# Filler matrix products around the first modulation rows of a one-core transformer step

## The chip, the cores and the metric

The kernel runs on one NeuronCore of one Trainium2 chip. A core has a tensor engine for matrix products (PE; its weight loads are listed apart as PEld), a vector engine (DVE), a scalar engine (ACT), a general engine (GpSimd, POOL) and a sync engine (SP) that issues most of the loads and stores. The engines run side by side, each through its own list of instructions in order, and wait for each other through semaphores. Matrix products write to PSUM, which the kernel uses as banks of 128 x 512 numbers; everything else lies in SBUF. Loads and stores go through sixteen DMA engines.

The metric is the device time of one execution in microseconds; lower is better. Times "before" are the median of three executions. A profile is a separate, single execution with a trace.

## The reference

The reference is one inference step of a small transformer layer with two kinds of tokens: 128 context tokens and 1,024 latent tokens, each with 1,024 features. All arithmetic is in float32. Cut to its core:

```
mod = silu(cond) @ w_ada + b_ada              # conditioning -> shift, scale, gate (3 x 1024)
h   = rmsnorm(x, norm_g) * (1 + scale) + shift
u, v, g_a, c_q, c_kv, k_rope, g_b = split(h @ w_in)
a_out = gelu(u) * (w_s @ rmsnorm(gelu(v)) + b_s) * silu(g_a)     # group A: mixing in chunks of 128
q     = rmsnorm(c_q) @ w_uq;  ckv = rmsnorm(c_kv)                # group B: latent attention, 4 heads
attn  = softmax(q_nope k_nope + q_rope k_rope) @ v               # latent tokens also read 256 cached keys
y     = x + gate * (concat(a_out, attn * silu(g_b)) @ w_o)
out   = rmsnorm(y, final_g)
```

There are two conditioning vectors, one for latent tokens and one for context tokens. The kernel returns the two outputs and the new latent and rope keys of the context tokens.

## The kernel before, in words

Tokens are handled as nine tiles of 128 (`x0` to `x8`), in three groups of three. Features are handled as eight chunks of 128, `k` = 0 to 7. Big products are made exact enough by splitting both factors into a high part (in a reduced format) and a low part (the rest) and adding three products: high by high, high by low, low by high. This document is about the first 50 us, in which each chunk goes through these steps:

- The sync engine loads x tiles, two halves of the modulation weights of a chunk (`ada`, 512 KB each, L447) and the value weights of the chunk (`wvr`, 256 KB, L308). The order of the queue is x0 to x2, ada of chunk 0, wvr0, x3 to x5, ada1, wvr1, ada2, wvr2, ada3, wvr3, ada4, wvr4, x6 to x8, ada5, wvr5, and so on. A load into a slot that is used again waits until the slot's last reader is done.
- `mod_rows` (L336) multiplies the conditioning with the modulation weights: four products per half, each writing 32 of the 128 rows of one PSUM bank, `modp`. `mod_copy` (L340, DVE) copies the result, `mod_cols` (L344, PE) turns it into columns, and `mod_act` (L347 and L348, ACT) makes the shift and scale of the chunk out of them.
- The x tiles are squared (L382 ACT, L384 DVE), the inverse roots are made (L399 to L403, DVE), and the tiles are scaled (L388 ACT, L392 DVE, L390 POOL).
- PE transposes the scaled tiles by chunk (L352). `xT` are the transposes used at once, `xe` are those of the first group for chunks 1 to 7, made ahead and copied out of PSUM by L523 (DVE and ACT), which frees the bank.
- ACT writes the high part of the modulated chunk (`hh`, L560) and the full value (`hf`, L567, or L569 on DVE); DVE makes the low part out of both (L112).
- POOL splits the value weights: L115 high, L534 low. (For chunk 0 ACT makes the high part, L528.)
- PE adds the value products: L421 and L422 (high parts) and L426 (low part).

The order on each engine is written when the kernel is built, by a small planner (`Plan`). Each step is added with an engine, a cost, the steps it needs and a priority; `run` walks through the planned time and issues the first step in order of priority that is ready. Costs and start times of the planner set only the order of instructions; on the chip the engines then wait by semaphore.

At the very start, before any data is there, PE multiplies a constant matrix by the identity `WARM0` = 24 times (`keep_warm`, L615 to L619) into a PSUM bank named `warm`. Nothing reads that result. The planner starts after it, with PE free from 8.2 us of its own clock (L622). The first planned PE steps are `rows0.0` and `rows0.1` (L576 and L577), the two halves of the modulation rows of chunk 0, then `cols0`, then the first transposes.

## Time and profile before

| what | value |
|---|---|
| median of three executions | 621.02 us (620.98 to 623.31) |
| span of the profiled execution | 620.5 us |
| PE busy in the span | 606.8 us, 98% |
| DVE, ACT, POOL busy | 66%, 48%, 20% |
| share of PE in the chain that ended last | 93% |
| mean granted PE clock | 0.991 |
| read and written in device memory | 40.87 MB, 4.83 MB |

The profiled execution has no other time of its own than its span, from its first to its last instruction; the 0.5 us to the median is what lies around a span.

A page of the profile lists busy time by engine, the span in 40 slices, the DMA queues, the chain of work that ended last (followed back from the last instruction, each time to what released it), and the costliest groups of instructions. Further views cut the same trace: by stretches of time, as a timeline, as the chain in order of time, or by who waited for whom. A row of the timeline has start, duration, engine, source line, operation, the tiles it writes and reads, how many records are merged, and in brackets how long the engine was idle before and what ended that. One matrix product in full float32 stands as two records; a transpose, or a product of split parts, as one. "PEclk" is the share of full speed that was granted to PE's clock. The trace's record of it begins at its first change, so the first few microseconds read 1.00 whatever they were.

### The profile page before, as it was taken

The page shows a single profiled execution, that of the slowest core. Times are in us where ns is not written, and L with a number is a line of the kernel's source. Part 1 is how long each engine was busy: PE and PEld are TensorE (multiplying, and loading weights), DVE is VectorE, ACT ScalarE, POOL GpSimd, SP SyncE. Part 2 cuts the span into 40 slices and gives each one's busy share as a digit, 9 for nine tenths or more (in the row PEclk, how much of TensorE's full clock was granted, in tenths as well). Part 3 has the DMA queues.
Part 4 walks back from the last instruction along what each step waited for, and adds up shares of the span by engine and source line. Part 5 has one row for each costly group of instructions (what it writes and reads, how often), then busy time and mean ns, then how long its engine had stood idle before and what let it go on. Part 6 is the DMA issues. An engine that isn't in the chain of part 4 may idle for free.

```text
span 620.5 us, 9955 instructions
## 1 busy us (share of the span) xinstructions
PE 606.8 (98%) x3719; PEld 549.0 (88%) x3719; DVE 411.3 (66%) x938; ACT 298.9 (48%) x694; POOL 123.2 (20%) x167
## 2 busy tenths in 40 slices
PE   7999999999999999999999999999999999999995
PEld 6777889999989999999998899999999988888884
DVE  4685457997756468566778656767666754577655
ACT  6556764345433245455675565555555632232212
POOL 2461112000000000433364112323222241000001
PEclk8999999999999999999999999999999999999998
DMA  8992010100351133100010000000101113423311
GB/s 316 393 380 71 0 35 2 35 0 3 134 208 70 64 106 122 38 1 1 1 42 1 1 2 0 2 9 27 35 1 35 35 68 129 144 101 137 115 55 68
DMA packets 15327, 46.32 MB, mean 75 GB/s; under 512 B 1824, under 2 KB 4784, under 8 KB 14768
## 3 DMA queue, kind: packets, MB, share of 16 engines
q1 hardware_dynamic: 15136, 45.50, 20.7%
q8 instruction: 29, 0.48, 0.3%
q10 hardware_dynamic: 144, 0.20, 0.1%
q14 instruction: 18, 0.15, 0.1%
HBM read 40.87 MB, written 4.83 MB: 74 GB/s over the span
## 4 chain that ended last, share of the span: by engine, by line
PE 93%; DVE 3%; DMA 1%; ACT 1%; issue 1%; SPq 0%; ACTq 0%
PE p L953 10%; PE tp L751 8%; PE tp L975 5%; PE pT L1550 5%; PE w L1797 5%; PE w L1799 5%; PE w L1798 5%; PE s L1505 3%; PE s L1506 3%; PE s L1504 3%; PE s L1503 3%; PE o L1574 3%; PE s L1507 3%; PE o L1576 3%; PE o L1575 3%; PE zacc L1389 2%
## 5 line engine op out<-in xcount | busy, mean ns | idle before, releaser
L112 DVE TENSOR_TENSOR pl<-pT,ph 128x512 fp32r<-128x512 f32 x81 | 55.4, 687 | 48.8 <-ACT ph L1554 48.2
L1488 ACT ACTIVATE e<-s,nb,scl 128x256 f32<-128x256 f32 x64 | 56.1, 881 | 35.1 <-DVE nb L1482 35.1
L1494 POOL TENSOR_SCALAR e<-e,rs 128x1280 f32<-128x1280 f32 x32 | 43.0, 1343 | 130.2 <-DVE rs L1493 124.7
L1554 ACT CAST ph<-pT 128x512 fp32r<-128x512 f32 x80 | 45.5, 588 | 41.9 <-PE pT L1550 39.0
L751 PE MATMUL tp<-area,w 128*128 128x384 f32 x288 | 52.5, 338 | 0.0
L751 PEld LDWEIGHTS tp<-area,w 128*128 128x128 f32 x288 | 50.4, 188 | 0.4
L1550 PE MATMUL pT<-ident,e 128*128 128x128 f32 x320 | 48.0, 272 | 1.3 <-DVE pl L112 1.2
L1574 PE MATMUL o<-ph,vh 128*128 128x256 f32 x160 | 47.8, 299 | 0.0
L1576 PE MATMUL o<-ph,vl 128*128 128x256 f32 x160 | 44.9, 281 | 0.0
L1575 PE MATMUL o<-pl,vh 128*128 128x256 f32 x160 | 44.7, 280 | 0.0
L1799 PE MATMUL w<-area,ml 128*128 128x512 f32 (+1 forms) x114 | 43.2, 379 | 0.0
L1550 PEld LDWEIGHTS pT<-ident,e 128*128 128x128 f32 x320 | 37.4, 140 | 4.8 <-issue 1.6
L1478 DVE TENSOR_REDUCE m<-s 128x1 f32<-128x1024 f32 x32 | 38.9, 1217 | 1.5 <-PE s L1507 1.5
L1503 PE MATMUL s<-kch,area 128*128 128x512 f32 (+2 forms) x100 | 38.9, 389 | 0.0
L1236 POOL TENSOR_TENSOR kr<-z,rope 128x64 f32<-128x64 f32 x8 | 2.6, 321 | 172.0 <-ACT z L1245 172.0
L1506 PE MATMUL s<-krh,area 128*128 128x512 f32 (+2 forms) x100 | 35.4, 354 | 0.0
L1505 PE MATMUL s<-kch,area 128*128 128x512 f32 (+2 forms) x100 | 35.4, 354 | 0.0
L1504 PE MATMUL s<-kcl,area 128*128 128x512 f32 (+2 forms) x100 | 35.3, 353 | 0.0
L1507 PE MATMUL s<-krl,area 128*128 128x512 f32 (+2 forms) x100 | 35.1, 351 | 0.0
L975 PE MATMUL tp<-area,w 128*128 128x384 f32 x192 | 35.0, 337 | 0.0
L975 PEld LDWEIGHTS tp<-area,w 128*128 128x128 f32 x192 | 33.6, 188 | 0.4 <-issue 0.4
L1574 PEld LDWEIGHTS o<-ph,vh 128*128 128x128 f32 x160 | 30.1, 188 | 1.6
(375 smaller groups left out, 1601.1 us busy)
## 6 DMA issues: line engine op xcount, KB each, us to landing
ada<-in_ada_ss SPq DMA_DIRECT2D x16, 512.0 KB, 8.1
w2r<-in_w_t SPq DMA_DIRECT2D x12, 512.0 KB, 4.4
x<-in_x SPq DMA_DIRECT2D x9, 512.0 KB, 7.4
xr<-in_x SPq DMA_DIRECT2D x9, 512.0 KB, 4.0
adag<-in_ada_g SPq DMA_DIRECT2D x4, 1024.0 KB, 4.8
wor<-in_w_o SPq DMA_DIRECT2D x8, 512.0 KB, 3.4
out_y<-y SPq DMA_DIRECT2D x8, 512.0 KB, 4.8
wvr<-in_w_v SPq DMA_DIRECT2D x8, 256.0 KB, 9.2
```

The source lines that it names most:

```text
L112: V.tensor_tensor(lo, src, f32(hi), op=ALU.subtract)
L751: T.matmul(tps[i, g][:, :GW], w_[i][:, k, :], x_[k, g], start=k == 0 and j == 0, stop=k == NK - 1 and j == 2)
L953: T.matmul(banks[key], a_, b_, start=k == 0 and m == 0, stop=k == 3 and m == len(passes) - 1)
L975: T.matmul(tps[c, 2][:, :GW], w_[c][:, k, :], x_[k, 2], start=k == 0 and m == 0, stop=k == NK - 1 and m == 2)
L1488: S.activation(e[:, sl], src, AF.Exp, bias=nb, scale=scl[:, t : t + 1], accum_out=su[:, i : i + 1])
L1503: T.matmul(ps, qh_, kch[:, sl], start=True, stop=False)
L1505: T.matmul(ps, ql_, kch[:, sl], start=False, stop=False)
L1550: T.transpose(ps[:, w : w + P], es[t, h][:, c * P : (c + 1) * P], ident)
L1574: T.matmul(o, vh[:, kt, :], ph[:, sl], start=c == 0, stop=False)
L1575: T.matmul(o, vh[:, kt, :], pl[:, sl], start=False, stop=False)
L1576: T.matmul(o, vl[:, kt, :], ph[:, sl], start=False, stop=c == n - 1)
L1799: T.matmul(ps, b, woh[k][:, c0:c1], start=False, stop=k == NK - 1)
```

## The change

The 24 products at the start become 29. Two further products of the same kind are issued right behind each half of the modulation rows of chunk 0, as part of the planner's steps `rows0.0` and `rows0.1`; the planned cost of these steps stays 0.45. To make this possible, the bank `warm` and the function `keep_warm` move ahead of `start_steps`; the bank is allocated at the same place in the order of banks as before. Everything else, and the order of instructions on every other engine, stays as it was.

```diff
-WARM0 = 24
+WARM0 = 29
...
+    warm = psa.tile([P, 512], F32, tag="acc", name="warm")
+
+    def keep_warm(n):
+        for _ in range(n):
+            T.matmul(warm[:, 0:P], ident, ones, start=True, stop=True)
+
     def start_steps(plan):
...
             if k == 0:
+                def warm_rows(i):
+                    mod_rows(0, i)
+                    keep_warm(2)
+
                 for i in range(2):
-                    step(f"rows0.{i}", "T", 0.45, lambda i=i: mod_rows(0, i), [f"ada0.{i}", *(["rows0.0"] if i else [])], 1)
+                    step(f"rows0.{i}", "T", 0.45, lambda i=i: warm_rows(i), [f"ada0.{i}", *(["rows0.0"] if i else [])], 1)
...
     with tc.manual_schedule(engines=engines):
-        warm = psa.tile([P, 512], F32, tag="acc", name="warm")
-
-        def keep_warm(n):
-            for _ in range(n):
-                T.matmul(warm[:, 0:P], ident, ones, start=True, stop=True)
-
         keep_warm(WARM0)
```

## The prediction

> **What bounds the kernel now.** I read the page first: which engine is busy, and what makes up the chain that ended last.

> ```profile
> span 620.5 us, 9955 instructions
> ...
> PE 606.8 (98%) x3719; PEld 549.0 (88%) x3719; DVE 411.3 (66%) x938; ACT 298.9 (48%) x694; POOL 123.2 (20%) x167
> ...
> PEclk8999999999999999999999999999999999999998
> ...
> PE 93%; DVE 3%; DMA 1%; ACT 1%; issue 1%; SPq 0%; ACTq 0%
> ```

> TensorE (PE) is the bound: 98% busy, 93% of the chain. Only its work, its clock or its waits can move the end. The clock row is low in the first slice and at the end only. So the view by stretches comes next, cut where the clock changes (columns: length, then busy time of PE, weight loads, VectorE, ScalarE and GpSimd, granted clock, DMA share, GB/s; x counts records).

> ```profile
> 4.96:8.37 3.41, 3.41 (x32) 3.41 (x32) 1.48 (x4) 1.23 (x3) 0.00 (x0) 1.00 1.04 327
> 8.37:11.78 3.41, 1.58 (x19) 0.46 (x18) 1.69 (x7) 2.37 (x5) 1.35 (x1) 1.00 1.01 383
> 11.78:15.19 3.41, 3.03 (x14) 3.03 (x15) 2.59 (x4) 2.12 (x6) 1.50 (x2) 0.50 1.03 419
> 15.19:18.60 3.41, 3.41 (x13) 2.93 (x12) 2.98 (x10) 2.28 (x5) 0.00 (x0) 0.50 1.03 404
> 18.60:22.01 3.41, 3.34 (x32) 2.13 (x30) 1.25 (x3) 1.77 (x3) 1.90 (x2) 1.00 1.03 402
> 22.01:25.42 3.41, 3.08 (x29) 1.96 (x29) 2.15 (x3) 3.17 (x7) 1.90 (x2) 1.00 1.03 404
> ...
> 25.42:48.50 23.08, 23.08 (x175) 16.63 (x173) 19.88 (x33) 12.05 (x27) 14.84 (x14) 1.00 0.92 348
> ```

> The clock is halved from 11.78 to 18.60 us, twice 3.41, right behind a stretch in which PE was busy for only 1.58 of 3.41 us (46%). It comes back behind a full stretch. At most half of 6.82, 3.41 us, is lost there. The DMA engines are full throughout (share 1.0), so loads will not land earlier.

> The third view is the timeline there (start, duration, engine, line, operation, out<-in, count, and what ended the wait before it).

> ```profile
> 1.36 7.32 PE L617 MATMUL warm<-ones,ident 128*128 128x128 f32 x48 [1.36 <-DVE onesr L239]
> ...
> 9.80 0.64 PE L336 MATMUL modp<-ada,csp 128*32 128x256 f32 x8 [1.12 <-DMA ada<-in_ada_ss]
> ...
> 10.97 0.64 PE L336 MATMUL modp<-ada,csp 128*32 128x256 f32 x8 [0.54 <-DMA ada<-in_ada_ss]
> ...
> 12.16 1.02 PE L344 MATMUL modp<-sel,rows 128*128 128x2 f32 x4 [0.55 <-DVE rows L340]
> ...
> 14.02 0.67 ACT L560 ACTIVATE area<-xT,at 128x384 fp32r<-128x384 f32 x1 [0.30 <-PE xT L352]
> ...
> 15.85 0.56 DVE L112 TENSOR_TENSOR area<-hf,area 128x384 fp32r<-128x384 f32 x1
> ...
> 16.32 1.02 DVE L523 COPY mixA<-xe 128x384 f32<-128x384 f32 x2
> ...
> 18.37 0.16 DVE L403 SCALAR_TENSOR_TENSOR x3r<-x3t,x3r 128x3 f32<-128x3 f32 x1
> ...
> 18.75 0.62 POOL L115 TENSOR_SCALAR w1t<-wvr 128x512 fp32r<-128x512 f32 x1 [5.18 <-DMA wvr<-in_w_v]
> ...
> 21.32 0.42 DVE L340 COPY rows<-modp 128x256 f32<-128x256 f32 x1 [0.47 <-PE modp L336]
> ...
> 21.66 1.41 DVE L392 TENSOR_SCALAR x<-x,x3r 128x1024 f32<-128x1024 f32 x2
> ...
> 23.12 0.66 PE L352 MATMUL xT<-ident,x 128*128 128x128 f32 x4 [0.33 <-DVE x L392]
> 23.16 0.62 POOL L115 TENSOR_SCALAR w1t<-wvr 128x512 fp32r<-128x512 f32 x1 [2.43 <-DMA wvr<-in_w_v]
> ```

> **The change, part by part.** *Five more fillers ahead (29 for 24).* A product is two records (24 gave 48). At full clock 32 records stand in 3.41 us, 0.107 us each. Ten more take 1.07 us: the last ends at 8.68 + 1.07 = 9.75. The first rows wait for their load until 9.80, so the cost is nothing, with 0.05 us of cover; any longer, and they push the first rows one for one.

> *Two more behind each half.* Four records are 0.43 us. The first half ends at 10.44 and its fillers at 10.87 at the latest; the second half waits for its load until 10.97. The second pair ends at 11.61 + 0.43 = 12.04; the column products wait for the copied rows until 12.16. That copy waits for the count raised by the second half's last row product, and the pair stands behind it. Cost nothing, cover 0.10 and 0.12 us. All other engines and the DMA queues (SP's and POOL's) keep their order: no load, copy or wait is moved.

> *What they fill.* From 8.37 to 11.78 PE is then busy for 1.38 (to 9.75) + 0.64 + 0.43 + 0.64 + 0.17 = 3.26 of 3.41 us, 96% instead of 46%. Whether that keeps the clock is read from the emptiest later stretch of this length in which it stayed full, until the work ends:

> ```profile
> 339.46:342.87 3.41, 2.46 (x23) 2.29 (x21) 2.49 (x6) 1.61 (x4) 1.33 (x1) 1.00 0.00 0
> ```

> There 72% was enough. So I take 11.78 to 18.60 at full clock. [...]

> *What full clock is worth.* The chain of waits (start, length, what) gives cold and warm prices of the same work:

> ```profile
> 13.92 2.56 PE xe L352 x12
> 16.48 0.43 PE vacc L421
> ...
> 18.90 0.70 PE vacc L426 x3
> 19.60 0.65 PE xe L352 x6
> 20.25 1.05 PE modp L336 x16
> ...
> 23.78 1.00 PE modp L336 x16
> ...
> 25.45 0.23 PE vacc L421
> ...
> 27.19 0.39 PE xT L352 x3
> ...
> 48.95 0.61 PE modp L344 x4
> ```

> From 12.16 on, warm: columns 0.61 (to 12.77), xT 0.39 (13.16), twelve xe at 0.65/6 = 0.108 each, 1.30 (14.46; before 16.48). The high half on ScalarE (L560) stood ready at 14.02 - 0.30 = 13.72 and waited for xT; the columns come 0.41 earlier, so it runs from about 13.3 to 14.0, in time. Six value products of 0.23 end at 15.84, before 18.90. Here 3.06 us are won, and given back step by step:

> - The low products wait for VectorE's L112, done at 16.41; ahead of it stand squares that start with a load, not with PE. Start 16.45 for 18.90: gain 2.45, end 17.14.
> - The next six xe need banks that L523 frees up to 17.34; they end at 17.80. Rows of chunk 1 follow. Their load stands just ahead of the w_v load that POOL gets at 18.75 (128x512 f32, 256 KB, 0.65 us at 404 GB/s): landed by 18.10, in time for their second half. Rows from 17.80 for 20.25: still 2.45.
> - Their copy stands on VectorE behind the root steps (to 18.53) and one L523 (1.02/2 = 0.51): 19.04 for 21.32, gain 2.28. The scaling behind it (L392) moves along, and xT goes on at 20.84 for 23.12.
> - Rows of chunk 2: second half by PE at 23.78 - 2.28 + 0.50 = 22.00, but its load stands just ahead of the w_v load seen at 23.16: 23.16 - 0.65 = 22.51. Before 24.28: gain 1.77.

> After that PE was busy without a gap to 48.5 us (last row of the stretches), so no more than 1.77 can be carried on. Late next is VectorE at the third group of x:

> ```profile
> 33.30 1.21 DVE L384 SCALAR_TENSOR_TENSOR junk<-x 128x1024 bf16<-128x1024 f32 x1
> ...
> 36.60 0.72 POOL L115 TENSOR_SCALAR w1t<-wvr 128x512 fp32r<-128x512 f32 x1 [4.98 <-DMA wvr<-in_w_v]
> ...
> 37.65 1.23 DVE L399 TENSOR_SCALAR x3v<-ssq 128x3 f32<-128x3 f32 x1
> ...
> 40.37 0.43 DVE L340 COPY rows<-modp 128x256 f32<-128x256 f32 x1
> ...
> 41.41 0.50 PE L344 MATMUL modp<-sel,rows 128*128 128x2 f32 x4
> ```

> Counted back from 36.60 over the loads between (256 KB and three of 512 KB, 0.65 + 3 x 1.30), x7 lands at 32.05. Its square at 33.30 can win 1.25 at most. VectorE works through from there to the fifth row copy, which ends at 40.80 and which PE needs at 41.41 - 1.77 = 39.64. At 40.80 - 1.25 = 39.55 that just holds. But L399 took 1.23 us where its like took 0.16: something held VectorE until 38.88. If scaling and copy (0.71 + 0.43) come behind that time again, PE goes on at 40.06: gain 1.35. If nothing moves there, at 40.84: 0.57. I take 1.5, between 1.35 and 1.77 and off the low end, since L399 would itself start 1.25 earlier. Behind 50 us PE's waits are few (the 93% above), and the gain reaches the end.

> Sum: the profiled span 620.5 becomes 619.0. The median of the runs, 621.02, lies 0.5 above that span, so 619.5 us (-0.24%).

> **The rivals.**
> *The cold stretch only moves: slower.* With work done sooner, PE waits for VectorE and loads instead. From 18.60 to 22.01 I count 0.25 of rows, 0.33 xe, 0.61 columns, 0.66 xT and 0.5 rows, 2.35 us, just under the 2.46 that held and well above the 1.58 that did not. If the clock halves at 22.01, dense work loses 1.7 us per stretch: one gives 621.2, two 622.9, three 624.6. From the first on it is slower than before. For it speaks that 3.03 of 3.41 us did not bring the clock back at 15.19; only a full stretch did. Chance 0.18, half of it with three stretches.

> *Transposes do not count as work: cold from 15.19.* Much of the 3.03 us of 11.78 to 15.19 was xT and xe, and the clock stayed down. Without them the new stretch there holds 0.26 of fillers, 0.61 of columns and 0.73 of value products, 1.60 us, as little as the 1.58 that failed. Until 18.60 it is then cold: value products still end about when L112 does; low products take 1.29 (17.74), four xe 0.213 each, two 0.108 (18.81), rows of chunk 1 start there for 20.25. That gain of 1.44 replaces 1.77 as the cap: 619.6 to 619.9. Chance 0.06. [...]

> *All of it comes back*, 3.41 us: 617.6. Against it stand the two load landings. Chance 0.12.

> *It does nothing*: the clock still drops at 11.78, since row products fill 32 of 128 columns (128*32 in their row) and may count for less: 621.0. Against: 96%. Chance 0.10.

> **How the numbers follow.** Forecast 0.54: 619.5, own range 619.2 (gain 1.77) to 620.5 (0.57). Over all cases the range is 617.8 to 622.9, leaving out the full recovery's lower half and three cold stretches. 0.5% is 3.1 us, about what a measurement of this kernel can tell from no change; within it lie 617.9 to 624.1. Faster 0.12 (full recovery), slower 0.10 (three stretches 0.09, fillers far over their cover 0.01), same 0.78.

> **What would show it.** Right: granted clock 1.00 from 8.37 to beyond 25 us; fillers ending near 9.75, rows still at 9.80 and 10.97; the first value product near 14.5; chunk 2's rows waiting for a load near 22.5. Wrong: clock 0.50 anywhere between 11.8 and 30 us, first rows later than 9.9, or PE waiting for VectorE over 0.5 us near 40 us.

## The result, and the profile after

| | median | lowest to highest | executions |
|---|---|---|---|
| before, on the same chip | 621.05 us | 620.06 to 623.31 | 13 |
| after | 623.75 us | 621.89 to 625.75 | 13 |

The changed kernel takes 1.0034 times as long as before, with a 95% interval of 1.0021 to 1.0047: about 2.1 us more (the two medians alone stand 2.7 us apart). The forecast was 1.5 us less, 619.5 us, and its range ended at 622.9. The difference is smaller than the 0.5% that the prediction set as its bound for a change, but it is clear of zero.

The profiled execution of the changed kernel took 622.97 us, and its span is 621.2 us, so 1.8 us lie around a span. With that, the profiled execution of before (span 620.5 us) took some 622.3 us. It stood above its median, not 0.5 us below it.

The head of the page after, and then its view by stretches, cut where the clock's own grid of 3.41 us lies in this execution. (The changes of the clock that the profiles of before and after record lie whole multiples of 3.41 us apart: before at 4.96, 11.78, 18.60 and 615.94 us, 2, 2 and 175 times; after at 4.25, where the record begins, and 618.65 us, 180 times.) The columns are length, then busy time of PE, weight loads, VectorE, ScalarE and GpSimd, granted clock, DMA share, GB/s:

```profile
span 621.2 us, 9991 instructions
...
PE 606.8 (98%) x3737; PEld 548.1 (88%) x3737; DVE 411.9 (66%) x938; ACT 299.0 (48%) x694; POOL 124.0 (20%) x167
...
PE 91%; DVE 4%; DMA 2%; issue 1%; ACT 1%; SPq 0%; ACTq 0%
```

```profile
4.25:7.66 3.41, 3.41 (x33) 3.41 (x32) 1.48 (x4) 1.15 (x2) 0.00 (x0) 1.00 1.04 354
7.66:11.08 3.42, 2.66 (x27) 2.09 (x26) 1.33 (x6) 1.95 (x4) 0.37 (x1) 1.00 0.98 343
11.08:14.49 3.41, 3.41 (x33) 2.78 (x33) 1.83 (x3) 2.45 (x6) 2.51 (x2) 1.00 1.03 422
14.49:17.90 3.41, 3.07 (x16) 1.94 (x14) 3.38 (x9) 2.75 (x6) 0.00 (x0) 1.00 1.03 402
17.90:21.32 3.42, 3.35 (x31) 1.75 (x29) 2.63 (x8) 2.42 (x5) 1.45 (x2) 1.00 1.03 403
21.32:24.73 3.41, 2.07 (x23) 1.26 (x23) 2.19 (x3) 2.64 (x5) 2.37 (x3) 1.00 1.03 389
24.73:28.14 3.41, 3.41 (x32) 2.34 (x30) 2.61 (x5) 0.00 (x0) 2.32 (x3) 1.00 1.00 321
```

In this execution the clock is full from 4.25 us on, and PE works as long in all as before (606.8 us). So the change did what it says, and still the span is 0.7 us longer. The timeline after shows where the gain went (start, duration, engine, line, operation; the brackets name the wait ahead). Lines below L426 keep their numbers; behind it they move by 6 (L534 is now L540), and from about L620 on by 4 (L1039 is now L1043).

```profile
1.36 8.11 PE L432 MATMUL warm<-ones,ident 128*128 128x128 f32 x58 [1.36 <-POOL ident masks.py:199]
10.23 0.64 PE L336 MATMUL modp<-ada,csp 128*32 128x256 f32 x8 [0.76 <-DMA ada<-in_ada_ss]
10.80 0.71 PE L432 MATMUL warm<-ones,ident 128*128 128x128 f32 x4
11.44 0.64 PE L336 MATMUL modp<-ada,csp 128*32 128x256 f32 x8
...
14.69 0.47 PE L421 MATMUL vacc<-w1t,area 128*128 128x512 f32 x1
...
18.48 0.64 PE L336 MATMUL modp<-ada,csp 128*32 128x256 f32 x8
...
19.78 0.62 POOL L115 TENSOR_SCALAR w1t<-wvr 128x512 fp32r<-128x512 f32 x1 [5.74 <-DMA wvr<-in_w_v]
...
20.12 2.49 DVE L392 TENSOR_SCALAR x<-x,x3r 128x1024 f32<-128x1024 f32 x2
...
20.49 1.58 POOL L540 TENSOR_TENSOR w1t<-wvr,w1t 128x512 fp32r<-128x512 f32 x1
...
22.67 0.66 PE L352 MATMUL xT<-ident,x 128*128 128x128 f32 x4 [1.34 <-DVE x L392]
...
184.63 1.07 PE L1043 MATMUL gps<-adag,csp 128*32 128x256 f32 x16 [0.56 <-DMA adag<-in_ada_g]
```

Up to 20 us it goes the way that was foretold, though less far: PE is up to 2.2 us ahead of before (3.06 were forecast), and at the rows of chunk 1 1.70 us (18.48 for 20.18; 2.45 were forecast). Then two steps take it back. VectorE's scaling of x4 and x5 (L392) starts 1.54 us sooner (20.12 for 21.66), but takes 2.49 us where it took 1.41, so it ends at 22.61 for 23.07 and PE's transposes go on only 0.45 us sooner (22.67 for 23.12). And at 184 us, far outside what the prediction looked at, PE waits for a load that it did not wait for before (the same product stood at 183.97, with no wait):

```profile
183.97 1.07 PE L1039 MATMUL gps<-adag,csp 128*32 128x256 f32 x16
```

From there to the end PE stays 0.66 us behind. This execution was one of the faster ones of the changed kernel, though; its median lies 0.8 us higher still. What the slower ones do has to come from experiments.

### The profile page after: what moved, and what is told of

It reads as the page before. It is cut to its first block, busy times and chain, and to the rows that moved or that the text cites. A ratio compares the mean times of both kernels' runs of the same rounds, so it can differ in the third digit from the quotient of the medians.

```text
span 621.2 us, 9991 instructions
## 1 busy us (share of the span) xinstructions
PE 606.8 (98%) x3737; PEld 548.1 (88%) x3737; DVE 411.9 (66%) x938; ACT 299.0 (48%) x694; POOL 124.0 (20%) x167
## 4 chain that ended last, share of the span: by engine, by line
PE 91%; DVE 4%; DMA 2%; issue 1%; ACT 1%; SPq 0%; ACTq 0%
PE p L957 9%; PE tp L755 8%; PE tp L979 5%; PE pT L1554 5%; PE w L1803 5%; PE w L1802 5%; PE w L1801 5%; PE s L1509 3%; PE s L1510 3%; PE s L1507 3%; PE s L1508 3%; PE s L1511 3%; PE o L1578 3%; PE o L1580 3%; PE o L1579 3%; PE zacc L1393 2%
## 5 line engine op out<-in xcount | busy, mean ns | idle before, releaser
L112 DVE TENSOR_TENSOR pl<-pT,ph 128x512 fp32r<-128x512 f32 x81 | 55.4, 687 | 48.9 <-ACT ph L1558 48.4
```

The costliest lines, as they stand in the source:

```text
L112: V.tensor_tensor(lo, src, f32(hi), op=ALU.subtract)
```

## The experiments

The theories. *Clock*: part of the executions get a half-clock window of 3.41 us at another, denser place. *Fetch*: the added products make PE's list of instructions longer, so that the blocks in which the chip fetches that list are fetched at other times and meet other loads. *Overrun*: the fillers end later than the load that they cover. In the expectations of the first four runs, theory A is the overrun, B is VectorE's scaling beside GpSimd, and C is a first profile that was not typical. The experiments of one batch ran on one chip with shared executions of the kernel before; ratios are against these.

### The parts, and both kernels again

The kernel before again; the change again; and each half of it. The fillers ahead alone, against before:

```diff
-WARM0 = 24
+WARM0 = 29
```

The pairs alone, against after:

```diff
-WARM0 = 29
+WARM0 = 24
```

> The kernel before, unchanged, once more, for the spread of its executions, their granted clock and a second trace. Its three first executions were 620.98 to 623.31 us and its one profile showed a halved clock from 11.78 to 18.60 us (mean clock 0.991 over the span). Theory A (the cold stretch is there in nearly every execution, and what slows the changed kernel is fillers that run over when the clock comes up late): mean clocks 0.989 to 0.993 in most executions, median 621.0. Theory B (the cold stretch costs little, since loads and VectorE cover it, and the changed kernel loses by moving VectorE's scaling of x onto GpSimd's weight split): the same clocks, median 621.0, and a time that does not follow the clock. Theory C (the profile was not typical, most executions have no cold stretch): clocks of 0.995 and more in most executions.

> The changed kernel, unchanged, once more on the same chip as its two halves: 622.9 to 624.6 us by its 13 executions, clock 0.991 to 0.998. Theory A: where the clock record starts late (a first full stretch that begins well after the first filler), the first rows start later than 10.2 us. Theory B: VectorE's two scalings of x near 20 us take over 2 us together, whatever the clock's start.

> Only the first part of the change: 29 fillers ahead, no pairs behind the halves. Busy share from 8.37 to 11.78 us would be 1.58 + 1.07 of 3.41 us, 78%, above the 72% that held the clock. Theory A: all of the slowdown is here, 623.0 to 624.5 us. Theory B: the clock is held, VectorE's scaling meets GpSimd's split as in the changed kernel, 621.5 to 623.7. If the five fillers cost nothing: 621.0.

> Only the second part: 24 fillers ahead, two products behind each half of the rows. Busy share from 8.37 to 11.78 us 1.58 + 0.43 + 0.17 of 3.41 us, 64%. Theory A: no slowdown, 620.0 to 621.3 us, since nothing stands ahead of the first rows that did not before. Theory B: as slow as the changed kernel where the clock is held, 621.5 to 623.7, and 621.0 where it is not.

Measured: before again 0.9991 (0.998 to 1.0002); the change again 1.0035 (1.0022 to 1.0047); the fillers alone 1.0023 (1.001 to 1.0036); the pairs alone 1.0017 (1.0007 to 1.0028). Each half costs about half. That is more than theory A allowed to the pairs, and it does not mean that each half has half of every cause: in neither half's profile does PE wait for adag, and the few executions of each with a full clock (mean .996 and more) have medians of 621.75 us (2) and 621.65 us (3), for 621.25 us of before in the same batch. The others have medians of 623.76 and 623.28 us. So the halves lose mainly where the clock falls. The profile of the change's repeat shows what the first one did not:

```profile
16.30:19.71 3.41, 3.07 (x28) 1.67 (x27) 2.88 (x11) 2.50 (x5) 0.00 (x0) 1.00 1.03 405
19.71:23.12 3.41, 2.00 (x16) 1.40 (x13) 3.08 (x4) 2.69 (x7) 2.37 (x3) 1.00 1.03 404
23.12:26.54 3.42, 3.42 (x22) 1.78 (x21) 1.57 (x4) 1.09 (x2) 2.35 (x3) 0.50 1.02 338
```

Here the grid of 3.41 us lies 1.8 us later (its first change is at 6.06 us for 4.25). The waits of 20 to 23 us fall into one stretch, 2.00 of 3.41 us busy (59%), and the clock halves behind it, over dense work. In the profile above the emptiest stretch, 21.32 to 24.73 us, was cut otherwise and had 2.07 us busy, and the clock stayed full. Over that cold stretch PE went from 0.51 us ahead of before to 0.99 us behind it, 1.5 us.

The grid thus has a part in it, and its place differs from execution to execution: the first recorded change of the clock lies between 4.25 and 7.52 us in all eighteen profiles but one (22.49 us, with the narrow fillers below). Busy time alone does not decide, though. The fillers alone, without the pairs, lost the clock behind a stretch of 2.20 us, more than the 2.07 that held above:

```profile
10.30:13.71 3.41, 2.20 (x25) 1.08 (x25) 1.80 (x6) 1.77 (x2) 1.97 (x2) 1.00 1.04 422
13.71:17.13 3.42, 3.42 (x17) 3.42 (x18) 3.17 (x5) 2.78 (x7) 0.90 (x1) 0.50 1.04 414
```

The mean granted clock of an execution tells the windows apart roughly, because one window costs 3.41 x 0.5 / 620 = .003 of it (and the end of the span, at half clock behind 615.94 us before and 618.65 us after, another .002 to .004): .996 and more is no window, .992 and less is two, between them it can be one or none. Taken so over all executions of the kernel before in these batches (135) and all of the change (18):

| mean clock | before: executions, median | after: executions, median |
|---|---|---|
| .996 and more | 48, 621.13 us | 5, 622.30 us |
| .993 to .995 | 37, 621.35 us | 9, 623.83 us |
| .992 and less | 50, 622.38 us | 4, 624.79 us |

Two things follow. Before has its cold stretch in about four executions of ten, not in all, and it costs 1.25 us there (622.38 less 621.13; 0.8 to 1.7 us batch by batch). The change, meant against that, has cold windows more often than not, and they cost it 1.5 us and more. And even without any window it is 1.2 us above before; this rests on five executions, which were not made beside those of before in the table. So there seem to be two costs.

### The list of instructions

33 narrower fillers in the kernel before, which were to last as long as its 24, with the change's length of list (33 products):

```diff
-WARM0 = 24
+WARM0 = 33
...
-                T.matmul(warm[:, 0:P], ident, ones, start=True, stop=True)
+                T.matmul(warm[:, 0:93], ident, ones[:, 0:93], start=True, stop=True)
```

And the change with 20 wider fillers (20 x 186 columns for 29 x 128), which with its pairs has the 24 products of before:

```diff
-WARM0 = 29
+WARM0 = 20
...
+    onesw = mixA[:, 3, 896:1152]
+    V.memset(onesw, 1.0)
...
-    def keep_warm(n):
+    def keep_warm(n, w=P):
         for _ in range(n):
-            T.matmul(warm[:, 0:P], ident, ones, start=True, stop=True)
+            T.matmul(warm[:, 0:w], ident, onesw[:, 0:w], start=True, stop=True)
...
-        keep_warm(WARM0)
+        keep_warm(WARM0, 186)
```

> The kernel before, with 33 narrower fillers (93 columns) in place of 24 of 128: the fillers last as long as before, but PE's list of instructions is as much longer as in the change, so all later PE instructions stand as far back in the list. Theory 'instruction fetch' (the longer list moves the moment at which a block of PE's instructions is fetched next to the gate load at 178 us, which then lands 1.3 us late): PE waits 0.5 to 1.2 us for adag near 184 us, and the median is 0.7 to 1.2 us above the kernel before, with the early clock as before. Theory 'clock' (the added products move a half-clock window from the load-bound first stretch to a later, denser one): no wait for adag of over 0.2 us, median within 0.4 us of the kernel before.

> The change, with 20 wider fillers (186 columns) in place of 29 of 128, and the two pairs kept: the fillers last as long as in the change, but with the pairs there are 24 products again, so PE's list has the length of before. Theory 'instruction fetch': no wait for adag near 184 us, the load lands within 5 us of its issue, and the median stands 0.9 to 1.3 us lower than the change's +2.1 us; if the fetch were all of it, it would equal the kernel before or beat it. Theory 'clock': still 1.5 to 2.5 us above the kernel before, with half-clock windows of 3.4 us after 13 us in more than half of the executions (mean clock .992 to .995).

The narrow fillers missed their purpose: 1.0108 (1.009 to 1.0126), 6.7 us more. They did not last as long as 24 wide ones, but until 15.75 us, and the clock came up only at 22.49 us (below, in the last section). That run says nothing on the list.

The 20 wide fillers gave 1.0010 (1.000 to 1.002): of 0.35% that the change costs, 0.25% are gone with the length of the list, 1.5 us (the products are wider as well as fewer, which no run separates). No wait for adag is left, although one such load still took 5.5 us where 5 were expected at most. The view of the DMA queues shows a likely cause (queue, then packets, MB and share of sixteen engines). q8 is a queue of instructions, which come in blocks of 16 KB (29 of 16,384 bytes in each of the profiles of before and after), and PE's list is the one that differs. Before, from 18 to 21 us and from 177 to 180 us:

```profile
q1 hardware_dynamic: 383, 1.18, 100.3%
q8 instruction: 1, 0.02, 2.2%
...
q1 hardware_dynamic: 81, 0.29, 34.6%
```

After, from 15 to 18 us and from 177 to 180 us:

```profile
q1 hardware_dynamic: 390, 1.19, 100.6%
q8 instruction: 1, 0.02, 2.3%
...
q1 hardware_dynamic: 113, 0.44, 57.3%
q8 instruction: 1, 0.02, 3.0%
```

The fetch of 18 to 21 us has moved ahead of 18 us (single records: 18.9 before, 16.2 after), and one that was at 184.3 us now runs from 178.3 to 179.7 us, into the first packets of the gate load (issued at 178.43 us, packets from 179.4). That load then takes up to 6.1 us for 4.8. The last line of the view of its tile, before and after:

```profile
DMA to landing us min/median/max: 4.8/4.8/5.0
```

```profile
DMA to landing us min/median/max: 4.8/4.8/6.1
```

A block takes 0.9 to 1.5 us in nearly all records, and 2.2% of sixteen engines over 3 us are 0.022 x 16 x 3 = 1.06 us: it is one packet, the time of one engine for about a microsecond. The gate load has sixteen landing records: after, fifteen of them stand by 183.30 us, the last at 184.49 us, and PE goes on at 184.63 us. In the packet records of after, four of the load's packets, which ran one behind the other for 0.31 us each, ended up to 1.2 us behind the others.

The records of all eighteen profiles bear this out for the third and the fourth of the four gate loads. Where a block of q8 ended 1.3 to 1.4 us behind the issue of the load (six loads), the load took 5.6 to 6.6 us. Where it ended 0.3 to 1.1 us behind the issue (twelve loads), the load took 4.7 to 5.1 us, with one exception of 5.6. But a block of q8 is not the only cause of a late load. The third took 5.5 to 5.8 us in six profiles without one in its time, that of the 20 wide fillers among them. In five of these, and in the exception, a block of 8 KB of another instruction queue (q14) fell into the first 3.7 us of the load, as it did in none of the undisturbed ones; that this is the reason was not tested.

### Filling the later gap

The other cost, the window behind 19.7 to 23.1 us, is tested by filling that gap too. First with five products ahead of the second group's transposes, in the bank of the fillers, with the change's fillers ahead and (second diff, on the wide fillers) with the list of before:

```diff
         def first_group():
+            keep_warm(5)
             h_pe(0, 1)
```

```diff
-WARM0 = 20
+WARM0 = 15
...
-        keep_warm(WARM0, 186)
+        keep_warm(WARM0, 247)
```

> The change, with five further fillers ahead of the second group's transposes near 21 us, where PE waits 1.3 us for VectorE's scaling. Theory 'clock': the stretch from 19.7 to 23.1 us then holds 1 us more of PE work, the clock stays full there, and the median falls by 1 to 1.5 us, to within 1 us of the kernel before. Theory 'instruction fetch': the list is longer again by five products, the fetch comes about 3 us sooner, clear of the adag load, and 1.2 us go for that reason: the wait for adag is then gone. A third way, the fillers overrun the scaled tiles: PE's xT later than 22.7 us, and 0.3 to 0.6 us worse than the change.

> Both repairs at once: the fillers of the change with five more near 21 us, but the 29 ahead as 15 of 247 columns, so that PE's list has the length of before (24 products). If 'clock' and 'instruction fetch' together make the loss, neither a half-clock window between 8 and 30 us nor a wait for adag is left, and the median is at or up to 1 us below the kernel before. If it still is more than 1 us above, a third cause is at work.

Measured: 1.0025 (1.0014 to 1.0035) and 1.0016 (1.0007 to 1.0025). All 23 executions have a mean clock of .996 or more: no window is left. But the time is 1.0 us or more above before all the same. PE's place is that of the expectation's third way, though the time is not worse than the change's. Holding the bank up to 21 us kept the early transposes (xe) from it, and the fillers ran over the scaled tiles:

```profile
19.21 0.55 PE L354 MATMUL xe<-ident,x 128*128 128x128 f32 x3 [0.57 <-ACT mixA L531]
...
21.77 1.36 PE L434 MATMUL warm<-mixA,ident 128*128 128x128 f32 x10
22.97 0.82 PE L354 MATMUL xT<-ident,x 128*128 128x128 f32 x6
```

These rows are of the second variant. PE comes to the transposes at 22.97 us, 0.3 us later than after. So the same again with three products, written where the next transpose writes over them, so that no bank is held, in the change and, with 17 fillers of 218 columns, on the list of before; and beside it the change with four fillers less:

```diff
         for j, t in enumerate(ts_):
+            if k == 0 and t in (4, 5):
+                for _ in range(6 - t):
+                    T.matmul(ps[:, j * P : (j + 1) * P], ident, ones, start=True, stop=True)
             T.transpose(ps[:, j * P : (j + 1) * P], x_block(t, k), ident)
```

```diff
-WARM0 = 20
+WARM0 = 17
...
-        keep_warm(WARM0, 186)
+        keep_warm(WARM0, 218)
```

```diff
-WARM0 = 29
+WARM0 = 25
```

> The change with three more products, between the transposes of chunk 0's second group (two ahead of x4's, one ahead of x5's), written into the bank that these transposes overwrite, so that no other bank is held longer (five in the warm bank had delayed xe by 1.0 us). Theory 'clock': no execution has a half-clock window before the end (mean clock .996 or more in all), and the median equals the change's executions without such a window, 621.9 to 623.0 us, about 1.4 us below its median. The fetch stays where the change has it (near 178.4 us), so 1 us above the kernel before is left. Theory 'fetch only': the clock is no cost, and the median stays at the change's +2.1 us.

> The same three products, with 17 fillers of 218 columns ahead and the pairs: 24 products in all, so that the instruction fetch lies where the kernel before has it. If half-clock windows and the fetch are the whole loss, all executions are as the ones without such a window in the variant of 20 wide fillers, 620.6 to 621.7 us, and the median is 0 to 0.5 us below the kernel before. If a third cause is at work, it is above it by 0.5 us or more.

> The change with 25 products ahead in place of 29, and its pairs: 29 products in all, as many as in the variant with 29 ahead and no pairs, whose instruction fetch lay at 184.3 us and not at 178.3 us. Theory 'instruction fetch': no wait of PE for adag near 184 us, the load lands within 5.0 us of its issue, median 0.8 to 1.3 us below the change, that is 0.6 to 1.4 us above the kernel before. Theory 'fillers and clock only': four fillers less are 0.43 us at full clock or 0.86 us at half clock and the rows still wait for the same load, so that the median stays within 0.4 us of the change's +2.1 us.

| kernel | products in the list | ratio (95%) | clock .996 or more |
|---|---|---|---|
| the change, again | 33 | 1.0035 (1.0022 to 1.0047) | 0 of 5 |
| the change, 25 ahead | 29 | 1.0026 (1.0011 to 1.004) | 4 of 9 |
| the change, 20 wide ahead | 24 | 1.0010 (1.000 to 1.002) | 4 of 12 |
| gap filled, 29 ahead | 36 | 1.0020 (1.0009 to 1.0032) | 11 of 11 |
| gap filled, 17 of 218 columns ahead | 24 | 1.0000 (0.9991 to 1.0009) | 11 of 11 |

The two costs add. With the gap filled the windows are gone in all executions; with the list of before the fetch is back, and with both the loss against before is gone. The list is worth 0.20% with the gap filled (36 against 24 products, with 3,712 and 3,706 columns ahead) and 0.25% without; the windows are worth 0.10 to 0.15%. In the profile of the long list with the gap filled, the wait for adag is 1.01 us, most of the list's 1.25 us:

```profile
185.05 1.07 PE L1046 MATMUL gps<-adag,csp 128*32 128x256 f32 x16 [1.01 <-DMA adag<-in_ada_g]
```

The rest may come from the first fetch, but no run separates it. The two profiles of the filled gap differ by 2.7 us in all, of which 0.8 lie ahead of 13 us, before either first fetch: the first load of weights landed at 10.28 us in one and 9.46 us in the other, by the landing records. It does so between 9.46 and 10.68 us in the eighteen profiles, so that a single pair of profiles can mislead. The expectation for 25 fillers failed in its size: the second fetch lay at 186.2 us and the wait for adag was down to 0.3 us, but only 0.09% of the 0.25% went, within the intervals of both. That 0.3 us stood without a block of q8 near the load. In its profile the first fetch still lies at 16.9 us, about as after.

The full repair only returns to the time of before. On the same chip before takes 620.75 us without a window (15 executions) and this kernel 621.10 us, which is not told apart: the fillers buy no more than what before loses to its cold stretch in four executions of ten.

### The scaling beside GpSimd, and the fetch moved on purpose

The scaling L392 slowed where it ran beside GpSimd's low split: 2.49 us after, 2.42 in its repeat, 2.45 with the gap filled and 24 products, for 1.41 before. It also took 1.41 us in the variant with 15 fillers, where it started behind the split. To take it away, ScalarE scales x4, in the variant with 20 wide fillers, in before and in the change; and in a fourth kernel with a still shorter list (11 fillers of 338 columns, one of 256 for each pair). The last of this batch is before with 12 fillers of 256 columns.

```diff
-SC1 = "SVV"
+SC1 = "SSV"
```

```diff
-WARM0 = 20
+WARM0 = 11
...
-                    keep_warm(2)
+                    keep_warm(1, 256)
...
-        keep_warm(WARM0, 186)
+        keep_warm(WARM0, 338)
```

```diff
-WARM0 = 24
+WARM0 = 12
...
-                T.matmul(warm[:, 0:P], ident, ones, start=True, stop=True)
+                T.matmul(warm[:, 0:256], ident, onesw, start=True, stop=True)
```

> The variant with 20 wide fillers and pairs (24 products), with ScalarE in place of VectorE scaling x4, so that VectorE has one scaling beside GpSimd's split of the value weights and not two. (The planner orders a few value products of chunk 1 otherwise for it.) Theory 'the early scaling meets the split': VectorE's two scalings took 2.08 to 2.49 us there for 1.41 us, and PE's second-group transposes came 0.7 to 1.1 us late; with ScalarE taking one, they end near 21.9 us for 22.8 us, the rows of chunk 2 wait for their load at 22.5 us, PE gains up to 0.5 us, and the median falls by 0.2 to 0.5 us against that variant. Rival 'ScalarE is full there': x4 comes at 21.2 us, but the copy of xe, the shift and scale of chunk 1 and the high part behind it each come up to 1.1 us later, and the median rises by 0 to 1 us.

> The kernel before with ScalarE in place of VectorE scaling x4, and nothing else but the planner's order of a few value products. Theory 'the early scaling meets the split': before, the two scalings start behind the split and take 1.41 us, so that there is no meeting to take away; the median stays within 0.5 us of before. Rival 'ScalarE is simply the better place for x4, whatever the clock': the 1.0 us that it gained on the variant of 20 wide fillers is gained here too.

> The change itself (29 fillers, pairs, 33 products) with ScalarE in place of VectorE scaling x4. It gained 2.4 us against the 24-product variant's 622.65 us (620.26 us), part of it by having no half-clock window in any execution. If the costs add, the half-clock windows go here too and the fetch's cost of 1.2 to 1.8 us stays: 621.5 to 622.1 us, at or up to 0.7 us above before, with PE still waiting about 1 us for adag near 184 us. If the fetch costs only where the scaling meets the split, 620.3 to 620.8 us.

> The variant with ScalarE scaling x4 (20 wide fillers, pairs of two, 620.26 us), with 11 fillers of 338 columns and one of 256 columns in place of each pair: 13 products of the same length in all. Theory 'the fetch follows the list': the first fetch comes later than 19.1 us by 1.5 to 4 us, behind the second half of chunk 2's modulation weights, which lands 1.2 us sooner (near 21.7 us), so that chunk 2's rows no longer wait for it: 0.3 to 1 us less, 619.3 to 620.0 us. Rival: the load that is late instead is as near to the bound, and the median stays within 0.3 us of 620.26 us.

> The kernel before with 12 fillers of 256 columns in place of 24 of 128: they last as long, and PE's list is shorter by 12 products. Theory 'the fetch follows the list': the first 16 KB fetch of PE's instructions, at 18.9 us before and at 16.2 us in the change, comes later by about as much as it came sooner there, near 21 to 23 us, and the jump in the spacing of the loads moves from the first half of chunk 2's modulation weights to a load behind it; the median changes by less than 0.6 us either way, since PE waits there for VectorE. Rival 'loads jump there for a reason of their own': the fetch moves and the jump stays at 18.7 to 21.1 us.

| kernel | products in the list | ratio (95%) | median |
|---|---|---|---|
| 20 wide ahead, ScalarE scales x4 | 24 | 0.9985 (0.9976 to 0.9994) | 620.26 us |
| the same, shorter list | 13 | 0.9989 (0.9977 to 1.0001) | 620.77 us |
| before, ScalarE scales x4 | 24 | 0.9993 (0.9981 to 1.0005) | 621.31 us |
| the change, ScalarE scales x4 | 33 | 1.0004 (0.999 to 1.0018) | 621.67 us |
| before, 12 wide fillers | 12 | 1.0001 (0.9989 to 1.0014) | 621.63 us |

The first of these is the only kernel that is clearly faster than before, by 0.15%, and so it beats both before and the change. It gains 0.25% on the same variant with VectorE scaling both tiles, more than the 0.2 to 0.5 us expected. Part of that is that all of its executions are free of cold windows (11 of 11, for 4 of 12); even so it lies 0.5 us below the executions of before without a window on its chip (620.75 us). Its rows:

```profile
19.56 1.27 POOL L542 TENSOR_TENSOR w1t<-wvr,w1t 128x512 fp32r<-128x512 f32 x1
19.82 1.56 DVE L394 TENSOR_SCALAR x<-x,x3r 128x1024 f32<-128x1024 f32 x1
...
21.44 0.66 PE L354 MATMUL xT<-ident,x 128*128 128x128 f32 x4 [0.37 <-DVE x L394]
```

One scaling alone beside the split takes 1.56 us, where two without it took 1.41. So the meeting is not gone; there is only one scaling left in it, and PE goes on at 21.44 us. Its fillers ran 0.8 us over their load (rows at 10.71 us for a load that landed at 9.78, where 0.14 us is the usual distance), and it is the fastest kernel all the same; so *overrun* seems to cost little. In the change itself ScalarE's scaling removes 0.31% of the 0.35%, and its profile has no wait for adag although the fetch is again next to that load (176.8 to 177.7 us, by the records): the load was issued at 176.85 us and its packets come about a microsecond later, just behind the fetch. The expected wait of about 1 us is thus missing, and the fetch seems to cost only where it overlaps the packets, which a shift of one microsecond decides. This profile is of one of the faster executions (620.76 us for a median of 621.67), so others may still wait. In before, ScalarE's scaling is not told apart from no change, so both theories on its place stay open there.

With 12 products ahead, the first fetch of before moved from 18.9 to 22.1 us, and the step in the landing of the loads with it: from 21 to 24 us

```profile
q1 hardware_dynamic: 382, 1.18, 100.3%
q8 instruction: 1, 0.02, 2.3%
```

By the landing records the first half of chunk 2's modulation weights came at 20.23 us for 21.13. That this first fetch follows the length of the list is thus shown in both directions. A later one need not: with 12, 24 and 29 products (the fillers alone) it lay at 184.4, 184.3 and 184.3 us. The time did not move by it (1.0001), so that load was not what PE waited for; and the shorter list gained nothing on the best variant either, against the expectation.

## Why the prediction was wrong, point by point

- *The clock stays full behind the first rows.* Right in the profile after, and in the place: the first value product at 14.69 us (forecast: near 14.5), rows of chunk 1 at 18.48 (17.80). Wrong in the repeat, where it fell at 23.12 us.
- *"The cost is nothing, with 0.05 us of cover"* (five fillers). The cost came true in both profiles of the change: the fillers ended at 9.47 and 10.33 us, and the rows started 0.13 us behind the landing of their load (10.23 for 10.10 us, 10.41 for 10.28), as in before (9.80 for 9.66). But the cover was luck: the load came late itself, and until the grid's first edge the fillers run at 0.213 us a record, by their starts in before and after; only behind it do they take 0.112 us, near the 0.107 us of the forecast. Where that edge lies at 7.36 us, the 24 of before already reach the rows. So it is in the kernel before with ScalarE scaling x4, whose start is that of before:

```profile
7.77 2.06 PE L617 MATMUL warm<-ones,ident 128*128 128x128 f32 x17
9.93 0.64 PE L336 MATMUL modp<-ada,csp 128*32 128x256 f32 x8
```

  With the change's own 29 fillers (ScalarE scaling x4) and an edge at 6.56 us the rows started at 10.50 us for a load of 9.97, and with the 20 wide ones and an edge at 7.52 us at 10.88 us for a load of 9.79, both without a wait.

- *What is there to win.* This is the first step that failed. The sum took the cold stretch of one profile for that of every execution. By the mean clock it stood in about four of ten, and cost 1.25 us there; so there were some 0.5 us to win on average, not 1.5. The place of the grid, which the sum took from that one profile, differed too: first edges from 4.25 to 7.52 us in seventeen of the eighteen profiles. The median's place fell too: "0.5 above that span" was 1.8 us around any span, so that the same gain would have given 620.8 us and not 619.5.
- *"No load, copy or wait is moved."* This step failed, with the largest price: 0.20 to 0.25%, 1.2 to 1.5 us. Order was kept, but the list grew by 36 instructions (9,991 for 9,955), and its fetches moved onto other loads. The nearest trace of it is in the sum itself: the second half of chunk 1's weights was to land by 18.10 us and landed at 19.03 (17.99 before, by the landing records), behind the first fetch, and its rows took 1.24 us for 1.07.
- *"The scaling behind it (L392) moves along."* It moved, into GpSimd's split, and took 2.49 us for 1.41. Of the 2.28 us forecast 0.45 was left in this profile. The split had been over before, so no row showed the price of the meeting.
- *"The gain reaches the end."* It did not: the wait for adag at 184 us cost 0.56 to 1.12 us in three profiles. The worry about the time near 40 us did not come true after (it stayed 0.45 us ahead up to 45 us, and a wait for a row copy at 48.7 us left 0.22), but was real where more gain came that far: the change with ScalarE scaling x4 was 2.35 us ahead of before at 28 us and 1.29 at 40 us, where PE waited 0.91 us for the row copy. (In that part of the prediction 38.88 + 0.71 + 0.43 is 40.02, not 40.06, which changes little.)
- *The rivals.* "The cold stretch only moves" is the part of the loss that the windows make, with 621.2 for one stretch; it held a chance of 0.18, and the mechanism was right: in the repeat the window behind 19.7 to 23.1 us costs 1.5 us (1.7 was forecast). "Transposes do not count" is refuted for these transposes: with the fillers alone, PE ran nothing but transposes from 13.82 to 16.74 us, in the half-clock stretch of 13.71 to 17.13 us shown above, and the clock was full behind it. The held 2.46 us that the argument leaned on was no threshold: 2.07 held too, while 2.20 did not.

## What to carry to other kernels

Work that is added to keep a clock up has to be judged over many executions, since the grid of the clock lay elsewhere from one to the next (first edges from 4.25 to 7.52 us here); a gap that is filled at one place may uncover the next one, as that of 19.7 to 23.1 us here. Instructions that wait for nothing still lengthen the list, and the longer list here moved its fetches against the loads (from 18.9 to 16.2 us, and from 184.3 to 178.3 us); where a wait appears far from an edit, look at the instruction queue. If a filler must be added, fewer and wider products keep the list as it was, which here was worth 0.20 to 0.25%.

## What the runs showed of the hardware

- In their profile the fillers of 93 columns did not raise the clock. 66 records lasted from 1.36 us for 14.39 us, 0.218 us each, about the 0.213 us that those of 128 columns take ahead of the first edge; and the clock was first seen to rise at 22.49 us, behind a stretch without such fillers. The timeline, and the stretches ahead of and behind the rise:

```profile
1.36 14.39 PE L617 MATMUL warm<-ones,ident 128*128 128x93 f32 x66 [1.36 <-DVE onesr L239]
```

```profile
12.25:15.66 3.41, 3.41 (x17) 3.26 (x16) 0.00 (x0) 0.05 (x1) 1.27 (x1) 1.00 1.03 418
15.66:19.07 3.41, 2.86 (x22) 1.51 (x21) 1.39 (x2) 0.00 (x0) 0.24 (x1) 1.00 1.03 404
19.07:22.49 3.42, 3.42 (x17) 3.42 (x18) 2.50 (x6) 2.76 (x7) 3.20 (x3) 1.00 1.04 405
22.49:25.90 3.41, 3.41 (x31) 2.53 (x30) 2.69 (x8) 2.12 (x5) 1.62 (x2) 1.00 0.55 213
```

  The first stretch is full of fillers by the view (and its 1.00 is the record not yet begun), and the clock was still not full in the next, where sixteen records of row products took 1.94 us for 1.07: a stretch that the records show as full was thus not enough to raise it.
- The clock came back behind stretches of transposes. In two of the six half-clock stretches behind which it came back (the fillers alone, 13.71 to 17.13 us, and before with 12 fillers), at most 0.6 of 3.41 us was anything else.
- One 16 KB block of instructions stands as one packet, of 0.9 to 1.5 us in nearly all records (0.88 to 1.43 us in before and after). Six 1 MB loads into which it ran for 1.3 to 1.4 us took 0.8 to 1.8 us longer than the usual 4.8.
- VectorE's scaling of 128 x 1024 numbers took 0.74 to 0.75 us alone (before again; two in 1.41) and 1.56 us beside GpSimd's 128 x 512 subtraction. In one profile, of the change with ScalarE scaling x4, it was the other way about: the scaling began 0.19 us ahead and took 0.74 us, and the subtraction 1.68 us for 1.27.
